# Other tiles for the second weight halves, for the b12 parts and for the first block's products in a stick-breaking decoder block

## The chip, the cores and the metric

The kernel runs on one core of one Trainium2 chip. The metric is the time of one execution in microseconds of the device. The kernel before has a median of 2233.52 us over three runs (2228.97, 2233.52 and 2234.57).

The core's engines are TensorE (PE, matmuls), VectorE (DVE), ScalarE (ACT), GpSimd (POOL) and SyncE (SP, which here issues nearly all DMAs). Each works through its own list of instructions in order and waits on semaphores for the others.

## The reference

One decoder block, 2048 tokens of width 1024, all in float32:

```
h = rmsnorm(x, g_mix_pre) * (1 + scale_m) + shift_m
mix = concat(stick_breaking_attention(q, k, v), pooling(u)) @ w_out     # q, k, v, u = h @ w_in
x = x + gate_m * rmsnorm(mix, g_mix_post)
h = rmsnorm(x, g_ffn_pre) * (1 + scale_f) + shift_f
f = (silu(h @ w_gate) * (h @ w_up)) @ w_down                            # 1024 -> 2816 -> 1024
x = x + gate_f * rmsnorm(f, g_ffn_post)
```

The change touches only the feed-forward part, from `h @ w_gate` and `h @ w_up` on.

## The kernel before, in words

**Precision.** A float32 product is made of three matmuls of rounded parts: each operand is split into a high part (ScalarE's rounding copy) and a low part (VectorE's difference), and `mm3` (lines 72 to 74) multiplies high by high, low by high and high by low. In the feed-forward part the split often goes through a PSUM bank (`split_by_bank`: L1169 the high part, L1176 a copy of it, L1177 the difference). A step of the plan is one group of such matmuls into one PSUM bank.

**Fast matrix products.** The feed-forward products `h @ w_gate` and `h @ w_up` are cut into 2 x 2 blocks (tokens by halves, features by halves, sums by halves), and are made by a Strassen-Winograd scheme in two levels: fewer block products, more additions of operands and results. The outer level has seven products. Four of them are made by an inner scheme of seven products each: these are the four groups `q` = 0 to 3 of `inner` (p1 to p4), each with 11 positions `j`, a position for 128 + 128 columns of gate and up. A position has seven steps of six matmuls, called a, e, f, b, h, i and d after their banks; d is put behind the first step of the next position. The other three outer products are made by `gate_up`, in 11 blocks of 12 steps with 12 matmuls each (`t_g`, `t_u`, `b_g`, `b_u` in the trace), which also takes up the four groups' results, makes silu and the product of gate and up, and the sums that the last product needs. Then `down` multiplies by `w_down` in the same manner, twice, and finishes the rows.

**The order of the work.** All steps stand in one list. The position m (0 to 43) of `inner` begins at step 7m - 1; `gate_up` begins at step 307. Each step carries what has to be done a number of steps ahead of it (`ahead`: loads, sums on GpSimd) and what is done with its bank one or two steps later (`take`). Beside the list a "side" generator makes the operands of the coming group, a piece a step: `main_operands` beside the fourth group, `rest_operands` from step 307 on. The order on TensorE, ScalarE, VectorE and GpSimd is the program's order. SyncE's DMAs are put in an order by the planner, which follows its own estimate of when each can go; on the chip that order is fixed, so a DMA that waits holds all behind it.

**Tiles.** Tiles come from pools by tag. A tag has a fixed number of buffers (`FT` for the pool `fx`); a new tile of a tag waits until an older one's last reader is done. What matters here:
- "s", six buffers: the results `p_c` of `inner` (`done`, L1384), which `keep` (L1380) stores two steps later to the DRAM tensor `pd`. In `rest_operands` four of them also hold b12 parts.
- "w320" and "w321" in the pools `ring` and `fx`: raw weights. Group q == 3 needs sums of two halves of the rows of the weights. The first halves (loaded at L1331) rotate over three tiles; the second halves (L1339) all go to one, "w321" of `ring`, but for the last position, whose second halves go to the two "cu" tiles. `row_sum` (L1342, GpSimd) adds the second half into the first, 10 steps (gate) and 9 steps (up) ahead of the position; the loads are issued 16 steps ahead. `s12` and `s34` (L1354 to L1360, GpSimd) follow at 8 and 7.
- "gf", one buffer of double width: a wide tile for several uses. "u2" and "u3", two buffers each: results of `take_p6` and `take_p7`, in `inner` and in `gate_up`.
- "gs" (three), "cu" (two), "u4" and "p1" (one each): token parts `hs` loaded by `token_part` (L1615) and intermediate results.
- `products_load` (L1426) loads four results of the groups from `pd`, 1 MB at once, into tiles `px` that rotate over "yah", "yal" and "y22", which until then hold operands of the fourth group.

The first gate/up block takes its weights (L1438) 21, 20, 17 and 11 steps ahead: gate's into both raw tiles of `ring`, up's into both of `fx`. In that block the first results are taken up in `take_p6`, where `u2g` (L1490) adds the first matmuls and a product from `px`. Five PSUM banks rotate there; bank 0 was the one of the last d step of the fourth group.

`down` (its slots of "u2" and "u3", and its load of `gfd` into "gf") and `combine` and `down_sums` are the rest of the code that the change's tiles touch.

Of the kernel before, what the change touches and what calls it, by code (L numbers as in the profile page):

```python
# [17 lines left out]
P = 128  # L18
# [3 lines left out]
HK = KC // 2  # L22
# [6 lines left out]
TB = 512  # L29
# [3 lines left out]
LAG = 2  # L33
OFF = 7
PRB = 6
FT = {"tr": 1, "gs": 3, "u4": 1, "gf": 1, "sr": 4, "s": 6, "u2": 2, "w320": 1, "u3": 2, "w321": 1, "p1": 1, "cu": 2}
WIDE = {"tr": 4, "gf": 2, "w320": 2, "w321": 2}
PAIRS, MAIN_PAIRS, HELD = 6, 4, 4
HELD_AT = (20, 12)
NQ = 4  # L40
# [7 lines left out]
def block_kernel(ctx, tc, x, c, w_cond, b_cond, g_mix_pre, g_mix_post, w_in, w_pool,  # L48
                 pool_scale, w_out, g_ffn_pre, g_ffn_post, w_gate, w_up, w_down, out):
    nc = tc.nc  # L50
# [1049 lines left out]
    for n in range(len(steps) + OFF):  # L1100
# [4 lines left out]
        if n < len(steps):  # L1105
            u, i = steps[n]
# [207 lines left out]
    def inner(q, j):  # L1314

        p = f"p{q + 1}"
        name = f"{p}_{j}"
        m = HF * q + j
        st = {}

        def load():
            if m == 0:
                st["g"], st["u"], st["s12"], st["s34"] = (t[:, n] for t in raw_pair(ring, name, (P, 2, TB)) for n in range(2))
            else:
                turn = 0 if m == 1 else (31 - m) % 4
                pool, n = ((fx, 1), (ring, 0), (fx, 0))[m % 3] if m >= 30 else (ring if turn > 1 else fx, turn % 2 == 0)
                w = ft("gf", f"{name}_32", (P, 2, TB)) if m == NQ * HF - 1 else raw_tile(pool, n, name, (P, 2, TB))
                st["g"], st["u"] = w[:, 0], w[:, 1]
            k0, f = ((0, j), (HK, j), (HK, j + HF), (0, j + HF))[q]
            for n, src in (("g", w_gate), ("u", w_up)):  # L1330
                (nc.scalar if m in (4, 5) else nc.sync).dma_start(st[n].rearrange("p (k n) -> p k n", k=HK), rows_of(src, k0, f))  # L1331
            if q == 3:
                if m == NQ * HF - 1:
                    st["g2"], st["u2nd"] = (ft("cu", f"{name}_2{n}") for n in "gu")
                else:
                    w = raw_tile(ring, 1, f"{name}_2", (P, 2, TB))
                    st["g2"], st["u2nd"] = w[:, 0], w[:, 1]
                for n, src in (("g2", w_gate), ("u2nd", w_up)):
                    nc.sync.dma_start(st[n].rearrange("p (k n) -> p k n", k=HK), rows_of(src, HK, f))  # L1339

        def row_sum(n, other):
            nc.gpsimd.tensor_tensor(st[n], st[n], st[other], ALU.add)  # L1342

        half = TB // 2
        one, two = slice(0, half), slice(half, TB)

        def sum_tile(n):
            if n not in st:
                st[n] = ft("sr", f"{name}_{n}")
            return st[n]  # L1350

        def s12():
            t, g, u = sum_tile("s12"), st["g"], st["u"]
            nc.gpsimd.tensor_tensor(t[:, one], u[:, one], u[:, two], ALU.add)  # L1354
            nc.gpsimd.tensor_tensor(t[:, two], t[:, one], g[:, one], ALU.subtract)

        def s34():
            t, g, u = sum_tile("s34"), st["g"], st["u"]
            nc.gpsimd.tensor_tensor(t[:, one], g[:, one], u[:, one], ALU.subtract)
            nc.gpsimd.tensor_tensor(t[:, two], g[:, two], st["s12"][:, two], ALU.subtract)  # L1360

        def step(w, part, v, vpart, bank, after, split_first=True):

            def split_w():
                if split_first:
                    pair = operand(f"{name}_{w}")
                    cols = two if w == "u" else slice(0, TB)
                    split_by_bank(*(t[:, cols] for t in pair), st[w][:, cols])
                    st[w + "r"] = [x.rearrange("p (k n) -> p k n", k=HK) for x in pair]

            def mm():
                st[bank] = (e_ps if bank in "de" else p_ps)(f"{bank}{name}")
                (wh, wl), (th, tl) = st[w + "r"], ys[p][v]
                mm3(st[bank], [((wh[:, 2 * part + k, :], wl[:, 2 * part + k, :]), (th[:, 2 * vpart + k, :], tl[:, 2 * vpart + k, :]))
                               for k in range(2)])

            return Step(1, split_w, mm, [(1, do) for do in after])

        def keep(kind, sb, t):
            nc.sync.dma_start(pd[sb][:, j, q // 2 * 4 + 2 * kind + q % 2, :], t)  # L1380

        def done(kind, sb, ps, rest):
            t = ft("s", f"{name}_c{kind}{sb}")
            nc.vector.tensor_tensor(t, ps, rest, ALU.add)  # L1384
            later(2, lambda: keep(kind, sb, t))

        def take_p1():
            st["p1"] = ft("p1", f"p1{name}")
            nc.scalar.copy(st["p1"], st["a"])

        def take_p5():
            st["u4"] = t = ft("gf" if not q and m and m % 2 == 0 else "u4", f"u4{name}")
            if not q:
                nc.scalar.copy(t, st["e"])

        def take_p6():
            st["u2"] = ft("u2", f"u2{name}")
            nc.vector.tensor_tensor(st["u2"], st["f"], st["p1"], ALU.add)
            if q:
                nc.vector.tensor_tensor(st["u4"], st["e"], st["u2"], ALU.add)  # L1400
            else:
                nc.gpsimd.tensor_tensor(st["u4"], st["u4"], st["u2"], ALU.add)

        def take_p7():
            st["u3"] = ft("u3", f"u3{name}")
            nc.vector.tensor_tensor(st["u3"], st["h"], st["u2"], ALU.add)

        r = [step("g", 0, "ya", 0, "a", [take_p1]),
             step("s12", 0, "v14", 0, "e", [take_p5]),
             step("s12", 1, "v32", 1, "f", [take_p6], False),  # L1410
             step("g", 1, "ya", 1, "b", [lambda: done(0, 0, st["b"], st["p1"])], False),
             step("s34", 0, "v32", 0, "h", [take_p7, lambda: done(1, 1, st["e"], st["u3"])]),
             step("u", 1, "v14", 1, "i", [lambda: done(1, 0, st["i"], st["u3"])]),
             step("s34", 1, "y22", 0, "d", [lambda: done(0, 1, st["d"], st["u4"])], False)]
        r[0].ahead = [({1: 9, 2: 12}.get(m, 16 if q == 3 else 14), load), (5 if m == 1 else 8, s12), (4 if m == 1 else 7, s34)]
        if q == 3:
            r[0].ahead += [(10, lambda: row_sum("g", "g2")), (9, lambda: row_sum("u", "u2nd"))]
        return r
# [2 lines left out]

    def products_load(n, sb, j):

        tag, pool = (("yah", "0r"), ("yal", "0r"), ("y22", "0b"))[next(px_turn) % 3]
        px[n, sb, j] = opools[pool].tile([P, 4, TB], F32, tag=tag, bufs=1, name=f"px{n}{sb}_{j}")
        nc.sync.dma_start(px[n, sb, j], pd[sb][:, j, 4 * n:4 * n + 4])  # L1426

    px_turn = itertools.count()

# [31 lines left out]
    def gate_up(j, at):  # L1461
# [24 lines left out]

        def take_p6(kind, sb, ps):
            p1, p2 = to_bank(0, kind, 0, sb), first(0, kind, 1, sb)
            u2 = st["u2", kind, sb] = ft("u2" if kind == "g" else "u3", f"u2{kind}{sb}_{j}")
            nc.vector.tensor_tensor(u2, ps, first(0, kind, 0, sb), ALU.add)  # L1490
            if kind == "g":
                gate("a11", sb, "sr", p1, p2)
            else:
                up("a11", sb, p1, p2)
# [115 lines left out]
                yield  # L1610
                yield

    def token_part(n, T0, tag, i):
        t = ft(tag, f"hs{T0}_{i}_{n}", (P, HK, P))
        nc.sync.dma_start(t, h2d[T0 + n % 2 * HK + i][:, n // 2 * HK:(n // 2 + 1) * HK, :])  # L1615
        return t

# [53 lines left out]
    def main_operands():  # L1671
# [18 lines left out]

        for u in range(2 * HK):
            t = 6 + 8 * u if u < 7 else 66
            tags = ("cu", "cu", "gf") if u in (1, 3, 5) else ("gs",) * 3
            for n, k, tag in zip((1, 3, 0), (6, 6, 5), tags):
                at(max(t - k, 0), lambda u=u, n=n, tag=tag: load(u, n, tag))
            at(t, lambda u=u: add(u, 1, 3, ALU.subtract))
            at(t + 1, lambda u=u: add(u, 0, 1, ALU.add))
            if u < HK:
                at(t + 2, lambda u=u: place(u, 1, "t3"))
                at(t + 4, lambda u=u: place(u, 3, "b22"))  # L1700
            at(t + 3 + 3 * (u < HK), lambda u=u: place(u, 0, "t2"))
# [5 lines left out]
    def rest_operands():  # L1707

        ops[1].update({n: pair_of(opools["0b"], tag, f"{n}_1") for n, tag in (("t3", "v14"), ("b22", "v32"))})
        b12 = [token_part(1, NTS, "s", i) for i in range(HK)]  # L1710
        b22 = [token_part(3, NTS, tag, i) for i, tag in enumerate(("gs", "gs", "gs", "p1"))]
        yield
        yield
        for k in range(HK + 2):
# [6 lines left out]

    def down(sb, dn):
        st = {}
        slots = ["s"] * 4 + ["u2", "u2", "u3", "u3"]
        wd_rows = w_down.rearrange("(i j p) n -> i p j n", p=P, i=2)
        quads = []

# [433 lines left out]
```

## Time and profile before

| | us |
|---|---|
| median of three runs | 2233.52 |
| lowest, highest | 2228.97, 2234.57 |
| profiled execution, its time | 2234.14 |
| its span, first to last instruction | 2232.4 |
| TensorE busy | 2180.1 (98%) |
| VectorE busy | 1669.8 (75%) |
| ScalarE busy | 1356.4 (61%) |
| GpSimd busy | 1217.4 (55%) |

The profile is of one execution. A line L72 in it is line 72 of the kernel file; since helpers record most matmuls, the tile's name tells which product it is (`ap` is bank a of a position, `t_g` a step of `gate_up`). In a line of the waits stand who waited, for whom, the total, the number of times and the longest. In a line in order of time stand the start, the duration, the engine, the line, the operation and output<-inputs, and in brackets the idle time before it and what ended it. Matmuls are pipelined: they are shown with 0.39 us each, though they begin every 0.23 us. SPq is SyncE's queue of DMA issues; its durations are those of the issue, not of the transfer.

### The profile page before, as it was taken

The page shows a single profiled execution, that of the slowest core. Times are in us where ns is not written, and L with a number is a line of the kernel's source. Part 1 is how long each engine was busy: PE and PEld are TensorE (multiplying, and loading weights), DVE is VectorE, ACT ScalarE, POOL GpSimd, SP SyncE. Part 2 cuts the span into 40 slices and gives each one's busy share as a digit, 9 for nine tenths or more (in the row PEclk, how much of TensorE's full clock was granted, in tenths as well). Part 3 has the DMA queues.
Part 4 walks back from the last instruction along what each step waited for, and adds up shares of the span by engine and source line. Part 5 has one row for each costly group of instructions (what it writes and reads, how often), then busy time and mean ns, then how long its engine had stood idle before and what let it go on. Part 6 is the DMA issues. An engine that isn't in the chain of part 4 may idle for free.

```text
span 2232.4 us, 34290 instructions
## 1 busy us (share of the span) xinstructions
PE 2180.1 (98%) x10349; PEld 1794.5 (80%) x10349; DVE 1669.8 (75%) x2552; ACT 1356.4 (61%) x2796; POOL 1217.4 (55%) x1700
## 2 busy tenths in 40 slices
PE   8999999999999999999999998799999999999998
PEld 6888888888888888878878876678888888887887
DVE  7874499999999965557787766597788775576566
ACT  5435599898989844457676655464444444455444
POOL 1452277787779965548887666556665520033003
PEclk9999999999999999999999999999999999999999
DMA  9986886534444456678899767889999997679553
GB/s 315 350 277 210 286 207 176 154 105 116 123 119 104 144 174 201 209 239 271 279 319 320 265 215 232 296 296 303 314 315 299 305 330 258 209 244 322 183 199 122
DMA packets 365622, 524.78 MB, mean 235 GB/s; under 512 B 24503, under 2 KB 204283, under 8 KB 357629
## 3 DMA queue, kind: packets, MB, share of 16 engines
q1 hardware_dynamic: 362876, 521.02, 71.7%
q8 instruction: 82, 1.34, 0.3%
q10 hardware_dynamic: 2560, 1.58, 0.3%
q14 instruction: 104, 0.84, 0.1%
HBM read 350.01 MB, written 172.49 MB: 234 GB/s over the span
## 4 chain that ended last, share of the span: by engine, by line
PE 45%; DMA 4%; DVE 4%; POOL 2%; issue 2%; ACT 2%; SPq 0%; DVEq 0%; POOLq 0%; ACTq 0%
PE dn0p L72 3%; PE dn0p L74 3%; PE dn0p L73 3%; DMA pd<-p_c 3%; PE dn1p L73 2%; PE dn1p L74 2%; PE dn1p L72 2%; PE t_u L74 2%; PE t_u L73 2%; PE t_u L72 2%; PE t_g L73 2%; PE t_g L72 2%; PE t_g L74 2%; PE mix L72 1%; PE mix L74 1%
## 5 line engine op out<-in xcount | busy, mean ns | idle before, releaser
L953 POOL TENSOR_TENSOR w<-sg,pr 128x512 f32<-128x512 f32 (+2 forms) x320 | 306.8, 959 | 46.1 <-DVE pr L948 13.5
L948 DVE TENSOR_TENSOR_SCAN pr<-pr,carry,begin 128x512 f32<-128x512 f32 x192 | 243.9, 1271 | 0.0
L932 ACT ACTIVATE sg<-z 128x512 f32<-128x512 f32 (+2 forms) x320 | 183.0, 572 | 50.9 <-PE z L930 40.5
L63 DVE TENSOR_TENSOR wtl<-wt,wth 128x512 fp32r<-128x512 f32 (+1 forms) x320 | 189.5, 592 | 17.9 <-ACT wth L62 15.8
L62 ACT CAST wth<-wt 128x512 fp32r<-128x512 f32 (+1 forms) x320 | 181.8, 568 | 10.4 <-PE wt L964 8.0
L934 ACT ACTIVATE pr<-z 128x512 f32<-128x512 f32 (+2 forms) x320 | 182.1, 569 | 0.0
L964 PE MATMUL wt<-ident,w 128*128 128x128 f32 x1088 | 172.3, 273 | 1.6 <-POOL pr L944 1.1
L964 PEld LDWEIGHTS wt<-ident,w 128*128 128x128 f32 x1088 | 134.0, 140 | 32.8 <-POOL pr L944 1.9
L1479 ACT ACTIVATE sa<-sa 128x512 f32<-128x512 f32 x88 | 54.9, 633 | 166.0 <-DVE sa L1478 162.6
L979 PE MATMUL av<-wth,vt 128*128 128x512 f32 (+1 forms) x320 | 126.1, 394 | 0.9 <-ACT o L984 0.8
L72 PE MATMUL dn0p<-w0p_h,g0p_h 128*128 128x512 f32 x308 | 119.8, 389 | 0.0
L73 PE MATMUL dn0p<-w0p_l,g0p_h 128*128 128x512 f32 x308 | 119.8, 389 | 0.0
L74 PE MATMUL dn0p<-w0p_h,g0p_l 128*128 128x512 f32 x308 | 119.8, 389 | 0.0
L929 PE MATMUL z<-kt,qt 128*128 128x512 f32 (+2 forms) x320 | 118.6, 371 | 0.7 <-ACT pr L934 0.6
L63 DVE TENSOR_TENSOR g0p_l<-g0p,g0p_h 128x512 fp32r<-128x512 f32 x77 | 59.3, 771 | 80.0 <-ACT g0p_h L62 80.0
L980 PE MATMUL av<-wtl,vt 128*128 128x512 f32 (+1 forms) x320 | 117.8, 368 | 1.3 <-DVE wtl L63 1.2
L930 PE MATMUL z<-kt,qt 128*128 128x512 f32 (+2 forms) x320 | 117.0, 366 | 0.0
L72 PE MATMUL dn1p<-w1p_h,g1p_h 128*128 128x512 f32 x292 | 113.7, 389 | 1.1 <-ACT w1p_h L62 1.1
L73 PE MATMUL dn1p<-w1p_l,g1p_h 128*128 128x512 f32 x292 | 113.8, 390 | 0.3 <-DVE w1p_l L63 0.3
L74 PE MATMUL dn1p<-w1p_h,g1p_l 128*128 128x512 f32 x292 | 113.6, 389 | 0.0
L945 DVE TENSOR_TENSOR_SCAN pr<-pr,zero,begin 128x128 f32<-128x128 f32 (+3 forms) x128 | 111.1, 870 | 1.7 <-ACT pr L934 1.7
L62 ACT CAST g0p_h<-g0p 128x512 fp32r<-128x512 f32 x77 | 48.0, 623 | 105.3 <-PE dn0p L73 90.3
(844 smaller groups left out, 7154.2 us busy)
## 6 DMA issues: line engine op xcount, KB each, us to landing
pd<-p_c SPq DMA_DIRECT2D x176, 256.0 KB, 4.8
px<-pd SPq DMA_DIRECT2D x44, 1024.0 KB, 7.3
hs<-h2d SPq DMA_DIRECT2D x80, 256.0 KB, 4.9
wc<-in_w_cond_dram SPq DMA_DIRECT2D x32, 512.0 KB, 7.4
qt<-qd SPq DMA_DIRECT2D x64, 256.0 KB, 4.0
p<-in_w_gate_dram SPq DMA_DIRECT2D x52, 256.0 KB, 4.9
p<-in_w_up_dram SPq DMA_DIRECT2D x52, 256.0 KB, 5.3
kt<-kd SPq DMA_DIRECT2D x96, 128.0 KB, 3.3
```

The costliest lines, as they stand in the source:

```text
L62: nc.scalar.copy(hi, src)
L63: low.tensor_tensor(lo, src, raw(hi), ALU.subtract)
L72: nc.tensor.matmul(ps, lh, rh, start=first and i == 0, stop=False)
L73: nc.tensor.matmul(ps, lh, rl, start=False, stop=False)
L74: nc.tensor.matmul(ps, ll, rh, start=False, stop=last and i == n - 1)
L929: nc.tensor.matmul(z[:, 0:L], qt[:, 0, i * P:(i + 1) * P], keys, start=True, stop=False)
L932: nc.scalar.activation(sg[:, 0:L], z[:, 0:L], AF.Sigmoid, scale=0.125)
L934: nc.scalar.activation(pr[:, 0:L], z[:, 0:L], AF.Sigmoid, scale=-0.125)
L948: nc.vector.tensor_tensor_scan(keys, keys, begin, carry, ALU.mult, ALU.bypass)
L953: nc.gpsimd.tensor_tensor(w[:, 0:L], sg[:, 0:L], pr[:, 1:L + 1], ALU.mult)
L964: nc.tensor.transpose(wt[:, i * P:(i + 1) * P], wss[u][i][:, b * P:(b + 1) * P], ident)
L979: nc.tensor.matmul(av[:, lo0:], vb, wh[:, lo0:], start=first, stop=False)
```

## The change

- The second weight halves of group q == 3 alternate: odd positions use "w321" of `ring`, even ones "gf" of `fx`; now the last position but one (m = 42) uses the two "cu" tiles, and the last (m = 43) "w321" of `ring`. Its first half stays in "gf".
- Of the four loads of a position in that group, the two of gate come first, then the two of up; before, the two first halves came first.
- `rest_operands` puts the b12 parts in one "cu" tile, two halves of a "gf" tile and "u4" instead of four "s" tiles, and issues each b12 load together with its b22 load.
- `products_load` begins its rotation with "yal" instead of "yah", and the loads with j = 0 and n = 0 (one for each half of the tokens) are made in two pieces of 512 KB.
- "u2" and "u3" have one buffer each, and "v2" and "v3" are new with one each. `inner` uses "u2" and "u3" alone; `gate_up` uses u for the first and v for the second half of the tokens; `down` uses all four; `main_operands` puts three of its parts in "v2" that were in "gf".

```diff
-FT = {... "u2": 2, "w320": 1, "u3": 2, ...}
+FT = {... "u2": 1, "v2": 1, "w320": 1, "u3": 1, "v3": 1, ...}
@@ inner, load
-            for n, src in (("g", w_gate), ("u", w_up)):
-                (nc.scalar if m in (4, 5) else nc.sync).dma_start(st[n].rearrange("p (k n) -> p k n", k=HK), rows_of(src, k0, f))
+            parts = [("g", w_gate, k0), ("u", w_up, k0)]
             if q == 3:
-                if m == NQ * HF - 1:
+                if m == NQ * HF - 2:
                     st["g2"], st["u2nd"] = (ft("cu", f"{name}_2{n}") for n in "gu")
                 else:
-                    w = raw_tile(ring, 1, f"{name}_2", (P, 2, TB))
+                    w = raw_tile(ring, 1, f"{name}_2", (P, 2, TB)) if m % 2 else ft("gf", f"{name}_2", (P, 2, TB))
                     st["g2"], st["u2nd"] = w[:, 0], w[:, 1]
-                for n, src in (("g2", w_gate), ("u2nd", w_up)):
-                    nc.sync.dma_start(st[n].rearrange("p (k n) -> p k n", k=HK), rows_of(src, HK, f))
+                parts = [parts[0], ("g2", w_gate, HK), parts[1], ("u2nd", w_up, HK)]
+            for n, src, k in parts:
+                (nc.scalar if m in (4, 5) else nc.sync).dma_start(st[n].rearrange("p (k n) -> p k n", k=HK), rows_of(src, k, f))
@@ products_load
-        tag, pool = (("yah", "0r"), ("yal", "0r"), ("y22", "0b"))[next(px_turn) % 3]
+        tag, pool = (("yal", "0r"), ("yah", "0r"), ("y22", "0b"))[next(px_turn) % 3]
-        nc.sync.dma_start(px[n, sb, j], pd[sb][:, j, 4 * n:4 * n + 4])
+        for k in range(0, 4, 2 if j + n < 1 else 4):
+            m = slice(k, k + (2 if j + n < 1 else 4))
+            nc.sync.dma_start(px[n, sb, j][:, m], pd[sb][:, j, 4 * n + m.start:4 * n + m.stop])
@@ gate_up, take_p6
-            u2 = st["u2", kind, sb] = ft("u2" if kind == "g" else "u3", f"u2{kind}{sb}_{j}")
+            u2 = st["u2", kind, sb] = ft("uv"[sb] + "23"[kind == "u"], f"u2{kind}{sb}_{j}")
@@ token_part
-    def token_part(n, T0, tag, i):
-        t = ft(tag, f"hs{T0}_{i}_{n}", (P, HK, P))
+    def token_part(n, T0, tag, i, t=None):
+        t = ft(tag, f"hs{T0}_{i}_{n}", (P, HK, P)) if tag else t
@@ main_operands
-            tags = ("cu", "cu", "gf") if u in (1, 3, 5) else ("gs",) * 3
+            tags = ("cu", "cu", "v2") if u in (1, 3, 5) else ("gs",) * 3
@@ rest_operands
-        b12 = [token_part(1, NTS, "s", i) for i in range(HK)]
-        b22 = [token_part(3, NTS, tag, i) for i, tag in enumerate(("gs", "gs", "gs", "p1"))]
+        b12, b22 = [], []
+        wide = ft("gf", "hs_wide", (P, 2, HK, P))
+        for i, (tag, tag2) in enumerate((("cu", "gs"), (None, "gs"), (None, "gs"), ("u4", "p1"))):
+            b12.append(token_part(1, NTS, tag, i, wide[:, (i - 1) % 2]))
+            b22.append(token_part(3, NTS, tag2, i))
@@ down
-        slots = ["s"] * 4 + ["u2", "u2", "u3", "u3"]
+        slots = ["s"] * 4 + ["u2", "v2", "u3", "v3"]
```

More of the change, by code (lines that the diff above doesn't have):

```diff
@@ L35 @@
 PRB = 6
-FT = {"tr": 1, "gs": 3, "u4": 1, "gf": 1, "sr": 4, "s": 6, "u2": 2, "w320": 1, "u3": 2, "w321": 1, "p1": 1, "cu": 2}
+FT = {"tr": 1, "gs": 3, "u4": 1, "gf": 1, "sr": 4, "s": 6, "u2": 1, "v2": 1, "w320": 1, "u3": 1, "v3": 1, "w321": 1, "p1": 1, "cu": 2}
 WIDE = {"tr": 4, "gf": 2, "w320": 2, "w321": 2}
```

## The prediction, as it went on record

> **What bounds the kernel now.** I read the page first, then the busy times by stretch, then the waits of TensorE, VectorE and SyncE's queue inside the weak stretch, then the time order of each engine there.
>
> ```profile
> span 2232.4 us, 34290 instructions
> PE 2180.1 (98%) x10349; PEld 1794.5 (80%) x10349; DVE 1669.8 (75%) x2552; ACT 1356.4 (61%) x2796; POOL 1217.4 (55%) x1700
> PE   8999999999999999999999998799999999999998
> ```
>
> TensorE is the bound. All that any edit outside the matmuls can win is its idle time, and the slices show where a lump of it lies, in the 8 and the 7 of slices 25 and 26 of 40. By stretches:
>
> ```profile
> 1140.00:1280.00 140.00, 140.00 (x619) 115.95 (x618) 112.53 (x187) 93.82 (x179) 105.75 (x118) 1.00 0.91 304
> 1280.00:1305.00 25.00, 23.36 (x101) 18.51 (x101) 17.63 (x30) 14.76 (x28) 19.57 (x22) 1.00 0.65 210
> 1305.00:1431.00 126.00, 111.65 (x466) 86.42 (x464) 82.25 (x136) 67.61 (x127) 78.28 (x80) 0.99 0.72 233
> 1431.30:1443.40 12.10, 12.10 (x53) 10.00 (x54) 4.30 (x7) 5.09 (x8) 3.00 (x3) 1.00 1.05 393
> 1443.40:1452.90 9.50, 0.39 (x2) 0.03 (x1) 0.84 (x2) 2.60 (x5) 6.89 (x6) 0.63 0.91 307
> ```
>
> The columns are length, then busy time with count of PE, PEld, DVE, ACT, POOL, then granted clock, DMA share and GB/s. From 1140 to 1280 (the second and third group of FFN products) PE never stops. From 1305 to 1431 lies the fourth group (q == 3), and PE is busy only 111.65 of 126; at 1443.4 it stands still for 9.5 us in the first gate/up block.
>
> ```profile
> 1305.54 0.39 PE L72 MATMUL ap<-yap4h,p_g_h 128*128 128x512 f32 x1
> ...
> 1314.83 0.39 PE L74 MATMUL ip<-v14p4h,p_u_l 128*128 128x512 f32 x1
> ...
> 1431.27 0.47 PE L72 MATMUL t_g<-t_0h,g_s_h 128*128 128x512 f32 x1 [0.53 <-DVE p_c L1384]
> ...
> 1443.40 0.39 PE L74 MATMUL t_u<-t_1h,u_s_l 128*128 128x512 f32 x1
> 1452.90 0.77 PE L72 MATMUL t_g<-t_0h,g_s_h 128*128 128x512 f32 x1 [9.11 <-DVE p_c L1384]
> ...
> 1457.23 0.39 PE L72 MATMUL t_u<-t_0h,u_s_h 128*128 128x512 f32 x1
> ```
>
> The first two rows are matmuls 1 and 42 of one position: 9.29 us over 41 spacings, 0.2266 us each, so a step of six takes 1.36 us and a position of seven steps 9.52 us. Four losses follow.
> - Tail of the third group: 25.0 us for 101 matmuls that need 22.9: 2.1 us.
> - Fourth group: 11 positions of 42 are 462 matmuls, 104.7 us; from 1305.54 to 1431.27 it took 125.7: 21.0 us.
> - Standstill: the matmul at 1443.40 should be followed at 1443.63; the next starts at 1452.90: 9.3 us.
> - Slow clock behind it: 12 matmuls from 1452.90 to 1457.23 take 4.33 us where 2.72 are due: 1.6 us.
>
> Together 34.0 us, the most that can go. Who causes them:
>
> ```profile
> SPq L1339 <- POOL p L1342: 39.1, 9, 6.5
> DVE p_c L1384 <- DMA pd<-p_c: 42.2, 14, 10.1
> POOL p L1342 <- DMA p<-in_w_gate_dram: 13.5, 4, 4.6
> POOL p L1342 <- DMA p<-in_w_up_dram: 10.5, 4, 6.0
> ```
> ```profile
> 1290.93 0.44 SPq L1380 DMA_DIRECT2D pd<-p_c  x1
> 1296.74 0.38 SPq L1339 DMA_DIRECT2D p<-in_w_gate_dram  x1
> 1297.21 0.93 SPq L1380 DMA_DIRECT2D pd<-p_c  x2
> 1298.20 0.49 SPq L1339 DMA_DIRECT2D p<-in_w_up_dram  x1
> ```
>
> Waits of 1280 to 1460 (total, times, longest). L1339 loads the second weight halves into one tile. Each load waits until GpSimd's row sum (L1342) of the position before has read it; SyncE's queue is in order, so the stores of the products (L1380) stand behind it, as between 1290.93 and 1296.74. The product tiles (tag "s", six) then don't come free, VectorE's next `p_c` waits, and with it the PSUM bank that PE wants. Nine holds of 39.1 us go with 2.1 + 21.0 us of loss: 0.59 us per us held.
>
> ```profile
> 1437.36 6.27 SPq L1615 DMA_DIRECT2D hs<-h2d  x5
> ...
> 1444.79 1.66 SPq L1380 DMA_DIRECT2D pd<-p_c  x1
> ```
> ```profile
> 1440.63 0.69 DVE L1490 TENSOR_TENSOR u2g<-t_g,px 128x512 f32<-128x512 f32 x1 [4.31 <-DMA px<-pd]
> 1452.06 0.69 DVE L1384 TENSOR_TENSOR p_c<-dp,u4p 128x512 f32<-128x512 f32 x1 [10.13 <-DMA pd<-p_c]
> ```
>
> The standstill has the same tail and another head: four of the six "s" tiles are given to b12 parts, so the last `p_c` must wait for a store that goes out at 1444.79, behind the `hs` loads. Its bank, 0, is what the next `t_g` needs.
>
> **The change, part by part.** The sum is made against the profiled execution's 2234.14 us, 0.03% above the median 2233.52.
>
> *Two tiles for second halves* (odd positions ring, even ones "gf", the last but one "cu"). A load now waits for the sum two positions earlier, 9.52 us more of slack against a longest hold of 6.5: the nine holds go, and 23.1 us with them. What is late next? At full pace the group's busy shares become POOL 78.28/104.7 = 75%, DVE 79%, ACT 65%, DMA 233 x 126/104.7 = 280 GB/s; from 1140 to 1280, with PE never idle, they are 76%, 80%, 67% and 304. No engine becomes the bound.
>
> *Gate's halves first.* The four issues and the stores between them took 3.7 us (1296.74 to the end of the last load issue); gate's pair is now out in about the first 1. Landing and sums:
>
> ```profile
> DMA to landing us min/median/max: 3.0/4.5/5.6
> L1342 POOL TENSOR_TENSOR p<-p,p x20: 1269/1291/1309, 1294.2 to 1399.6; 128x512 f32<-128x512 f32 x20
> ```
>
> The sums stand 6 and 7 steps behind the load, 8.2 and 9.5 us: gate's is due 6 to 7 us after the first issue, up's 8 to 9. It fits, up's barely; I count nothing gained here.
>
> *Two holds stay.* The "cu" pair for position 42 (step 277) was last read by an add that the side generator issues at the end of that same step; and the gate weights of the first block (step 286) now share the ring tile with position 43, whose sum stands at step 291. I take 2 us a hold, near one and a half steps of lag (0 if other work is queued ahead, 6.5 as before at worst): 2 x 2 x 0.59 = 2.4 us come back, 0 to 7.7.
>
> *b12 in "cu", "gf" and "u4".* "s" holds products alone, so the last `p_c` no longer waits for a store behind `hs` loads: 9.3 + 1.6 us go. The loads keep their number; five of eight find their tile free ahead of the block, the one in "u4" only after the last `p_c`, which frees it. What is late next for bank 0: VectorE is in order, and `u2g` waits for the products until 1440.63; that, one more addition and `p_c`, three of 0.69 us, end near 1442.7, still ahead of 1443.63.
>
> *First block's products in halves, tiles swapped.* Two more issues of about 0.5 us on SyncE; half of the bytes stand ahead of `u2g`. Swapping the tiles moves a release by one matmul (0.23 us). Counted at nothing: the 0.9 us between 1442.7 and 1443.63 cover the issues, and without that cover they cost their 1.0.
>
> *"v2" for the third main tile, "u2" and "u3" split.* In gate/up the rotation is as before. In the 44 positions u2 and u3 now have one buffer instead of two.
>
> ```profile
> L1398 DVE TENSOR_TENSOR u2p<-fp,p1p x11: 678/692/692, 993.2 to 1087.8; 128x512 f32<-128x512 f32 x11
> L1402 POOL TENSOR_TENSOR u4p<-u4p,u2p x11: 1289/1297/1312, 994.6 to 1088.7; 128x512 f32<-128x512 f32 x11
> ```
>
> GpSimd's reads start 0.9 to 1.4 us after the first and last writes and take 1.3; the next write is some 9.5 us off: no wait. This is the one read by another engine, and only the first group has it.
>
> *A new wait at the seam.* Weights, `hs` parts and products crowd there (393 GB/s). I take one wait of about 0.7 us, with a clock dip, whose price these rows give:
>
> ```profile
> 1328.86 0.47 PE L72 MATMUL ap<-yap4h,p_g_h 128*128 128x512 f32 x1 [1.86 <-DVE u2p L1398]
> ...
> 1329.88 0.63 PE L73 MATMUL ap<-yap4l,p_g_h 128*128 128x512 f32 x1
> ...
> 1332.87 0.57 PE L74 MATMUL dp<-y22p,p_s_l 128*128 128x512 f32 x1
> ```
>
> Seven spacings take 2.99 us instead of 1.59, 1.4 us lost behind a wait of 1.86. So 0.7 + 1.4 = 2.1 us (0 to 2.1 + 1.6). [...]
>
> Sum: 34.0 - 2.4 - 2.1 = 29.5 us; 2234.14 - 29.5 = **2204.6 us**.
>
> **Rivals.**
> - *The seam is bound by transfers.* During the standstill 9.5 us x 307 GB/s = 2.9 MB moved. If they are all needed without it, at 393 GB/s they take 7.4 us, with the dip 1.6: 2200.1 + 2.4 + 9.0 = 2211.5. For it: DMA share 1.05 ahead of the standstill. Against: five `hs` loads move ahead of the block, into a stretch with share 0.72.
> - *The fourth group is paced by landing.* GpSimd's 24.0 us of waits for weights (13.5 + 10.5) then stay. If up's sum is late by 1.5 us in each of 11 positions, 11 x 1.5 x 0.59 = 9.7 us stay: 2200.1 + 9.7 + 4.5 = 2214.3. For it: up's margin is under 1.5 us. Against: the loads go out on time once the queue isn't held.
> - *The holds move elsewhere.* SyncE's order is set by the planner; if `hs` loads waiting for "gs", "cu" or the shared ring tile hold the stores as L1339 did, the gain shrinks to a few us: about 2230.
> - *Slower: single u2.* In the first group VectorE's next write of u2 waits for GpSimd's read of the last. A wait of x in each of its 11 positions costs 11x; from x = (34.0 + 6.7)/11 = 3.7 us on the kernel is slower, at 4.5 us it takes 2200.1 + 4.5 + 49.5 = 2254. For it: GpSimd is in order, and a wait there for weights delays the read. Against: the read would have to end over 10 us later than the rows show. Elsewhere writer and readers are VectorE alone.
>
> **How the numbers follow.** Chances: forecast 0.62; transfers 0.17; landing 0.12; holds move 0.06; slower 0.03. A measurement of this kernel tells some 0.3% (6.7 us) from no change: the first three are faster (0.91), the fourth within (0.06), the last slower (0.03). The range runs from 2198 (all 34.0 gone and 0.1% of run to run) to 2215, which takes in the two middle rivals; outside are the last two and the edges, under 0.2.
>
> **What would show it.** Right: the wait of L1339 for L1342 near nothing; the waits of `p_c` for its stores fall from 42.2 to under 10 us; fourth group near 105 us; no wait of `t_g` for `p_c` of 9 us. The landing rival would show L1342 still waiting over 15 us for weights; the transfer rival a PE wait of several us in the first block for `px`, `hs` or weights with DMA share near 1; the slower one a wait of L1398 for L1402. I am wrong if the fourth group still takes over 115 us, or if PE loses time in a place where it does not today.

## The result and the profile after

The kernel after takes 2225.76 us (median of 16 runs, 2223.70 to 2228.95); the kernel before, beside it, 2234.52 us (16 runs). The ratio is 0.9961, with a 95% interval of 0.9954 to 0.9969. It is faster by 8.8 us where 29.5 were forecast, and lies above the range of 2198 to 2215. The profiled execution took 2223.88 us.

The page after, its span and TensorE's row of slices:

```profile
span 2222.1 us, 34293 instructions
PE   8999999999999999999999999899999999999998
```

Of the 8 and the 7 in slices 25 and 26 one 8 is left. Next come the stretches after (length, then busy time with count of PE, PEld, DVE, ACT, POOL, then granted clock, DMA share, GB/s): the tail of the third group, the fourth group, and the seam to the first gate/up block.

```profile
1280.00:1305.00 25.00, 23.04 (x99) 17.87 (x98) 17.85 (x30) 14.74 (x28) 19.80 (x22) 1.00 0.66 218
1305.00:1431.00 126.00, 112.38 (x466) 86.16 (x464) 81.32 (x135) 67.47 (x127) 77.44 (x79) 0.99 0.71 228
1431.00:1457.00 26.00, 23.89 (x103) 19.25 (x103) 20.02 (x31) 17.17 (x30) 12.02 (x10) 1.00 1.06 368
```

The seam is nearly full now. Before, the same stretch read:

```profile
1431.00:1457.00 26.00, 16.62 (x66) 13.34 (x67) 9.50 (x17) 10.43 (x17) 10.72 (x9) 0.80 0.92 325
```

37 matmuls more are 37 x 0.2266 = 8.4 us: nearly the whole gain of 8.8. The fourth group kept its 112 busy us of 126. The first matmul of the group and the first behind it, after:

```profile
1305.64 0.39 PE L72 MATMUL ap<-yap4h,p_g_h 128*128 128x512 f32 x1
...
1431.99 0.47 PE L72 MATMUL t_g<-t_0h,g_s_h 128*128 128x512 f32 x1 [0.99 <-DVE p_c L1384]
```

They stand 126.35 us apart, where before it was 125.7 and 104.7 were due. The waits after, from 1280 to 1460 (total, times, longest):

```profile
SPq L1339 <- POOL p L1342: 38.1, 7, 7.0
DVE p_c L1384 <- DMA pd<-p_c: 38.7, 17, 5.2
```

The hold that the second tile was to remove is there with 38.1 us in 7 waits, against 39.1 in 9. The time order shows why. In SyncE's queue before, L1339 is a load of second halves and L1331 one of first halves:

```profile
1296.74 0.38 SPq L1339 DMA_DIRECT2D p<-in_w_gate_dram  x1
...
1298.78 0.56 SPq L1331 DMA_DIRECT2D p<-in_w_gate_dram  x1
...
1307.01 0.37 SPq L1339 DMA_DIRECT2D p<-in_w_gate_dram  x1
...
1310.23 0.40 SPq L1331 DMA_DIRECT2D p<-in_w_gate_dram  x1
...
1319.08 0.38 SPq L1339 DMA_DIRECT2D p<-in_w_gate_dram  x1
```

After, the same queue (all four loads are now of line 1339; the second, 1298.86, and the fourth, 1309.91, are first halves), and GpSimd's row sums:

```profile
1296.82 0.38 SPq L1339 DMA_DIRECT2D p<-in_w_gate_dram  x1
...
1298.86 0.56 SPq L1339 DMA_DIRECT2D p<-in_w_gate_dram  x1
...
1306.75 0.37 SPq L1339 DMA_DIRECT2D p<-in_w_gate_dram  x1
...
1309.91 0.38 SPq L1339 DMA_DIRECT2D p<-in_w_gate_dram  x1
...
1319.26 0.38 SPq L1339 DMA_DIRECT2D p<-in_w_gate_dram  x1
```
```profile
1294.26 2.54 POOL L1342 TENSOR_TENSOR p<-p,p 128x512 f32<-128x512 f32 x2
1304.04 2.68 POOL L1342 TENSOR_TENSOR p<-p,p 128x512 f32<-128x512 f32 x2 [4.22 <-DVE p_s_l L1177]
...
1327.44 1.27 POOL L1342 TENSOR_TENSOR p<-p,p 128x512 f32<-128x512 f32 x1 [2.69 <-DMA p<-in_w_gate_dram]
...
1396.85 1.30 POOL L1342 TENSOR_TENSOR p<-p,p_2g 128x512 f32<-128x512 f32 x1 [5.44 <-DVE u2p L1398]
```

The issues stand at the same times to a few tenths; what they load is different. The order of the built program on SyncE names it, for the positions j = 0 to 3 of the group (gate's loads alone; "2nd" are second halves, in brackets what a load waits for, beside others):

```
before   1st j=0 | 2nd j=1 [sum of j=0] | 1st j=1 | 2nd j=2 [sum of j=1] | 1st j=2 | 2nd j=3 [sum of j=2] | 1st j=3
after    1st j=0 | 2nd j=2 [sum of j=0] | 1st j=1 | 2nd j=3 [sum of j=1] | 1st j=2 | 2nd j=4 [sum of j=2] | 1st j=3
```

(After, the second halves of j = 1 stand some 80 entries ahead of those of j = 0, and no sum holds them.) With two tiles a load of second halves waits for the sum two positions back. But the planner, which puts a load where it reckons its tile to come free, now places it one position earlier on the list. It still stands before the sum that is just being made, and the next position's first halves stand behind it, as before. So a ring is closed: a sum ends at 1306.72 (1304.04 and 2.68), the second halves go out at 1306.75, the first halves behind them at 1309.91, they land, and the next sums follow; the two of the next position end near 1319.2, and at 1319.26 the queue moves again. The brackets of GpSimd's rows name now the first halves (1327.44), now a VectorE operation. The landings settle it: of the positions 1 to 9 the trace has the landing of gate's first halves for j = 1, 5, 6, 8 and 9, and each time the sum begins 0.12 or 0.13 us later (j = 1: landed at 1303.91, begun at 1304.04). From the first gate sum to the tenth the ring takes (1396.85 - 1294.26)/9 = 11.40 us a position, where the matmuls need 9.52: 11 x 11.40 = 125.4 us, the length of the group.

### The profile page after: what moved, and what is told of

Same layout as the page of the kernel before. It is cut to its first block, busy times and chain, and to the rows that moved or that the text cites. A ratio compares the mean times of both kernels' runs of the same rounds, so it can differ in the third digit from the quotient of the medians.

```text
span 2222.1 us, 34293 instructions
## 1 busy us (share of the span) xinstructions
PE 2179.7 (98%) x10349; PEld 1794.8 (81%) x10349; DVE 1673.5 (75%) x2552; ACT 1355.9 (61%) x2796; POOL 1215.6 (55%) x1700
## 4 chain that ended last, share of the span: by engine, by line
PE 77%; DVE 6%; DMA 5%; POOL 4%; issue 3%; ACT 3%; SPq 1%; DVEq 0%; POOLq 0%; ACTq 0%
PE wt L964 4%; PE dn0p L73 3%; PE dn0p L74 3%; PE dn0p L72 3%; PE dn1p L72 3%; PE dn1p L73 3%; PE dn1p L74 3%; PE av L980 2%; PE z L929 2%; PE z L930 2%; PE av L979 2%; DMA pd<-p_c 2%; PE mix L72 2%; PE mix L74 2%; PE mix L73 2%
```

## The experiments

What was left to tell apart: does the order on SyncE (the loads behind the hold, the first halves above all) make the group slow, or do the stores behind the hold, as the prediction had it, or is one tile simply too few? And which of the three parts of the change brought the 8.8 us? Each run is compared with the kernel before on its own chip (medians 2232.65, 2233.08 and 2233.83). In the code shown, ... stands for lines left out.

**The parts alone.** Each is the kernel before with one part of the change.

`tiles_only`: the second halves on two tiles, gate's first, with "v2" and "v3".

```diff
...
-w = raw_tile(ring, 1, f"{name}_2", (P, 2, TB))
+w = raw_tile(ring, 1, f"{name}_2", (P, 2, TB)) if m % 2 else ft("gf", f"{name}_2", (P, 2, TB))
...
+parts = [parts[0], ("g2", w_gate, HK), parts[1], ("u2nd", w_up, HK)]
...
```

> The kernel before with the second weight halves on two tiles, gate's first, and with u2, v2, u3, v3 (main's three parts in v2); b12 parts and products as before. Theory A (the planner puts each load of second halves where its tile comes free in its own estimate, so a second tile moves the load one position earlier and SyncE still stands before it until the row sum just being made is done): no gain, 2232 to 2237 us, the fourth group still near 126 us, L1339 waiting some 38 us for L1342. Rival B (the two tiles do relieve the group, and the rest of the change gives it back): 2210 to 2220 us.

2237.06 us, ratio 1.0019 (1.0010 to 1.0029). The second tile alone gains nothing; if anything it costs 4 us, and what costs them stays open. Its waits from 1280 to 1460:

```profile
SPq L1339 <- POOL p L1342: 38.9, 7, 6.2
PE t_g L72 <- DVE p_c L1384: 9.2, 1, 9.2
```

Both losses of before are there.

`b12_only`: the b12 parts in "cu", "gf" and "u4".

```diff
-b12 = [token_part(1, NTS, "s", i) for i in range(HK)]
...
+wide = ft("gf", "hs_wide", (P, 2, HK, P))
+for i, (tag, tag2) in enumerate((("cu", "gs"), (None, "gs"), (None, "gs"), ("u4", "p1"))):
+    b12.append(token_part(1, NTS, tag, i, wide[:, (i - 1) % 2]))
...
```

> The kernel before with the b12 parts in cu, gf and u4, issued beside the b22 parts, and nothing else. Theory A: the whole gain of the change is here, 2224 to 2228 us, no wait of 9 us of t_g for p_c. Rival C (the standstill goes only if the products come earlier too): 2229 to 2234 us with a wait of u2g for px in its place.

2224.17 us, ratio 0.9967 (0.9956 to 0.9979): the gain of the whole change, within the interval.

```profile
SPq L1339 <- POOL p L1342: 37.1, 9, 6.7
PE t_g L72 <- DVE p_c L1384: 0.8, 1, 0.8
```

The hold is as before, and TensorE's 9 us of standstill are gone.

`products_only`: the first block's products in halves, the tiles swapped.

```diff
-(("yah", "0r"), ("yal", "0r"), ("y22", "0b"))[next(px_turn) % 3]
+(("yal", "0r"), ("yah", "0r"), ("y22", "0b"))[next(px_turn) % 3]
...
```

> The kernel before with the first block's products in halves and the tiles yal and yah swapped, nothing else. Theory A: no change, 2232 to 2237 us, the wait of 9 us stays because its store still goes out behind the hs loads. Rival C: 2227 to 2231 us.

2233.95 us, ratio 1.0006 (0.9997 to 1.0015): nothing, as counted.

**What the group could be.** `no_second_halves`: the kernel after without the loads of the second halves and their sums.

```diff
-parts = [parts[0], ("g2", w_gate, HK), parts[1], ("u2nd", w_up, HK)]
...
-r[0].ahead += [(10, lambda: row_sum("g", "g2")), (9, lambda: row_sum("u", "u2nd"))]
```

> The changed kernel without the loads of the second weight halves and without their row sums; this part of the computation is left out, so its time is a floor for the fourth group. Theory A (the hold of SyncE at these loads is what costs): the group takes 105 to 108 us and the kernel 2200 to 2207 us. Rival D (another bound holds the group: the stores, the first halves or the order on VectorE): the group over 115 us, the kernel over 2212 us.

2200.85 us, ratio 0.9867 (0.9850 to 0.9883). The group:

```profile
1304.69 0.39 PE L72 MATMUL ap<-yap4h,p_g_h 128*128 128x512 f32 x1
...
1409.41 0.39 PE L72 MATMUL t_g<-t_0h,g_s_h 128*128 128x512 f32 x1
```

104.7 us, the floor of the prediction: the whole loss of the group hangs on these loads and sums. This run does not say how.

**The order.** `pinned`: the kernel after, with the second halves bound to be issued behind the first halves of their own position. Tiles, bytes and sums stay.

```diff
-parts = [parts[0], ("g2", w_gate, HK), parts[1], ("u2nd", w_up, HK)]
-for n, src, k in parts:
+parts += [("g2", w_gate, HK), ("u2nd", w_up, HK)]
+for i, (n, src, k) in enumerate(parts):
+    with (tc.issue_after(loaded.ins) if i > 1 else ExitStack()):
+        loaded = (...).dma_start(...)
```

> The changed kernel with one more rule for the planner: a position's second halves are issued behind its first halves (issue order only, no wait for data). Theory A (the second tile was spent on issuing a position earlier; held to its place, the load meets a tile whose sum is long done): L1339's and L1340's waits for L1342 under 15 us, the group under 112 us, 2203 to 2212 us. Rival D (one position's sum, landing and next sum make a loop that no order shortens): group over 120 us, 2220 us or more.

2201.95 us, ratio 0.9863 (0.9849 to 0.9878). Its stretch of the fourth group, a wait, gate's loads in its queue (first halves of j = 1 and j = 2, second halves of j = 2, first and second halves of j = 3) and three sums:

```profile
1305.00:1411.00 106.00, 105.61 (x466) 87.21 (x465) 83.09 (x136) 67.94 (x127) 76.77 (x78) 1.00 0.85 269
```
```profile
DVE p_c L1385 <- DMA pd<-p_c: 7.5, 4, 3.3
```
```profile
1292.85 0.79 SPq L1340 DMA_DIRECT2D p<-in_w_gate_dram  x1
...
1300.59 0.38 SPq L1340 DMA_DIRECT2D p<-in_w_gate_dram  x1
...
1302.96 0.39 SPq L1340 DMA_DIRECT2D p<-in_w_gate_dram  x1
...
1307.92 0.38 SPq L1340 DMA_DIRECT2D p<-in_w_gate_dram  x1
...
1309.43 1.16 SPq L1340 DMA_DIRECT2D p<-in_w_gate_dram  x1
```
```profile
1308.80 2.55 POOL L1343 TENSOR_TENSOR p<-p,p 128x512 f32<-128x512 f32 x2 [1.67 <-DVE p_c L1385]
1316.85 2.55 POOL L1343 TENSOR_TENSOR p<-p,p 128x512 f32<-128x512 f32 x2
1325.02 2.56 POOL L1343 TENSOR_TENSOR p<-p,p 128x512 f32<-128x512 f32 x2
```

The first halves of j = 1 go out at 1292.85, where after they went out behind the hold at 1298.86; those of j = 2 at 1300.59 and not at 1309.91. The sums now come 8.1 us apart, faster than the 9.52 that TensorE needs, and TensorE is busy for 105.61 of 106 us. The order alone is worth 2225.76 - 2201.95, about 24 us, or 22.4 when each is taken against the kernel before of its own batch.

`by_scalar_queue`: the kernel after, with the second halves issued by ScalarE. Their wait then holds nothing on SyncE.

```diff
-(nc.scalar if m in (4, 5) else nc.sync).dma_start(...)
+(nc.scalar if m in (4, 5) or n in ("g2", "u2nd") else nc.sync).dma_start(...)
```

> The changed kernel with the second halves issued by ScalarE's queue, in program order, 16 steps ahead of the position, instead of SyncE's. Theory A: SyncE has no hold left there; group 105 to 110 us, 2201 to 2209 us. Rival E (the issue and its wait only move onto ScalarE, whose casts then come late): 2212 us or more, with waits of PE for the casts or copies of L1169 and L1176.

2203.15 us, ratio 0.9867 (0.9853 to 0.9882); the group takes 104.7 us (1307.24 to 1411.96). The same gain in another way. The time of the issues alone does not make it: the 22 issues moved last 10.2 us together, the longest being

```profile
1361.18 0.75 ACTq L1339 DMA_DIRECT2D p<-in_w_up_dram  x1
```

and 22.6 us are saved against the kernel after (21.2 when each is taken against the kernel before of its own batch), because what stood behind the wait no longer does: on SyncE no wait of L1339 for L1342 is left from 1280 to 1460, where after there were 38.1 us of it.

`first_halves_written_first`: the kernel after with both first halves written ahead of the second halves in the program, as before, and nothing bound.

```diff
-parts = [parts[0], ("g2", w_gate, HK), parts[1], ("u2nd", w_up, HK)]
+parts += [("g2", w_gate, HK), ("u2nd", w_up, HK)]
```

> The kernel after with one edit: in the program both first halves of a position are written ahead of both second halves again, with nothing that binds the planner. If the planner places a load where its tile comes free, whatever the order of writing, SyncE's list stays what it is, the fourth group takes 126 us and the time is 2226 us (2223 to 2229). If it was writing gate's pair ahead of up's that put the second halves of a later position in front, the group falls to 105 to 115 us and the time to 2202 to 2214.

2225.25 us, ratio 0.9959 (0.9946 to 0.9971): the order of writing changes nothing. The planner places the loads, and of the edit of `pinned`, which writes them in this order too, the binding is what gains.

**Stores or loads behind the hold.** `stores_by_scalar`: the kernel after with the fourth group's stores on ScalarE's queue. SyncE's holds then keep back only loads.

```diff
-nc.sync.dma_start(pd[sb][:, j, q // 2 * 4 + 2 * kind + q % 2, :], t)
+(nc.scalar if q == 3 else nc.sync).dma_start(pd[sb][:, j, q // 2 * 4 + 2 * kind + q % 2, :], t)
```

> The changed kernel with the fourth group's stores of products issued by ScalarE's queue; the loads stay on SyncE, held as before. Theory S (the cost comes through the stores behind the hold, the s tiles and p_c): waits of p_c for pd under 10 us, group under 112 us, 2203 to 2212 us. Theory F (it comes through the next position's first halves behind the hold: sum, issue, landing, next sum make a loop of 11.5 us): the group stays over 120 us, 2219 to 2228 us, and PE waits for s12 or the gate split instead of for p_c.

2227.23 us, ratio 0.9974 (0.9964 to 0.9983), no better than after. Waits, then SyncE's gate loads (second halves, first halves, second halves, from 1339 on), then the sums and two `hs` additions of GpSimd (L1687), which make operands for `gate_up`:

```profile
SPq L1339 <- POOL p L1342: 40.2, 9, 6.8
DVE p_c L1384 <- DMA pd<-p_c: 7.9, 4, 3.7
```
```profile
1339.50 0.37 SPq L1339 DMA_DIRECT2D p<-in_w_gate_dram  x1
...
1341.62 0.45 SPq L1339 DMA_DIRECT2D p<-in_w_gate_dram  x1
...
1351.32 0.37 SPq L1339 DMA_DIRECT2D p<-in_w_gate_dram  x1
```
```profile
1336.96 2.50 POOL L1342 TENSOR_TENSOR p<-p,p 128x512 f32<-128x512 f32 x2 [0.41 <-DVE p_s_l L1177]
...
1347.53 1.30 POOL L1687 TENSOR_TENSOR hs<-hs,hs 128x512 f32<-128x512 f32 x1 [1.21 <-DMA hs<-h2d]
1348.78 2.52 POOL L1342 TENSOR_TENSOR p<-p,p 128x512 f32<-128x512 f32 x2
...
1358.20 2.66 POOL L1687 TENSOR_TENSOR hs<-hs,hs 128x512 f32<-128x512 f32 x2 [3.87 <-DMA hs<-h2d]
1360.82 2.52 POOL L1342 TENSOR_TENSOR p<-p,p 128x512 f32<-128x512 f32 x2
```

VectorE's waits for stores fell from 38.7 to 7.9 us, and the kernel gained nothing: the sums still come 11.8 and 12.0 us apart, with no store on SyncE in these rows. So the stores behind the hold are not needed for the slow pace; the loads behind it are enough. This run does not part one kind of load from the other. At 1348.78 and 1360.82 gate's first halves had landed 0.5 and 1.2 us before the sum began, and what ended last was an `hs` addition, whose load is behind the hold as well. That the first halves set the pace in the kernel after is shown there, by their landings. The run is no clean one in two more respects: the last stores of the third group stay on SyncE until 1324, and ScalarE, with 44 issues more, now makes VectorE wait for its copies (15.9 us of `p_s_l`). The group takes 130.5 us (1306.16 to 1436.64), so its length is no measure of the hold alone. The rows used here are of the time after 1324.

**One tile or two.** `one_tile_pinned`: the kernel before, with one tile for the second halves, and the same binding of the order.

```diff
...
+with tc.issue_after(loaded.ins):
     nc.sync.dma_start(st[n].rearrange("p (k n) -> p k n", k=HK), rows_of(src, HK, f))
```

> The kernel before (one tile) with the same rule of issue order. Theory A (with one tile the sum just being made must still be awaited: hold, loads, landing of some 5 us, two sums of 1.3): the hold stays, group 115 to 126 us, 2224 to 2236 us. Rival F (only the first halves behind the hold cost): group under 112 us, 2214 to 2221 us, the standstill of 9 us at the seam left.

2208.14 us, ratio 0.9886 (0.9870 to 0.9903), faster than either expectation. The group takes 104.7 us (1302.50 to 1407.22); the standstill is left:

```profile
PE t_g L72 <- DVE p_c L1385: 7.8, 1, 7.8
```

`b12_one_tile_pinned`: the same with the b12 parts in the tiles of the change. `pinned_second_look` ran beside it, with the edit of `pinned`.

> The kernel before with two edits: the b12 parts in the tiles of the change, and the second halves of a position issued behind its own first halves. One tile for the second halves stays. If the place on SyncE's list is all that the fourth group needs, the second tile is worth nothing: the group takes 105 us, the standstill of 9 us is gone too, and the time is that of the pinned kernel, 2202 us (2200 to 2204). If the second tile does carry a part of the gain once the order is right (landing and the row sum then come one after the other in one tile), it is 2205 to 2212, with waits of GpSimd's row sum for the weights over 15 us and TensorE idle in the fourth group.

> The kernel after with the second halves issued behind their own position's first halves, as in the run pinned, beside the two others on the same chip: 2202 us (2200 to 2204). If the one-tile kernel of this batch is within 3 us of it, the second tile is worth nothing that can be measured here.

One tile: 2199.04 us, ratio 0.9844 (0.9831 to 0.9858). Two tiles, with the rest of the change: 2200.78 us, ratio 0.9853 (0.9839 to 0.9867). The intervals overlap; the second tile is worth nothing that can be measured. In the one-tile kernel the fourth group has no gap at all, though its sums still wait for gate's weights:

```profile
1305.00:1411.00 106.00, 106.00 (x469) 87.79 (x468) 83.89 (x138) 70.40 (x131) 79.26 (x80) 1.00 0.89 286
```
```profile
POOL p L1343 <- DMA p<-in_w_gate_dram: 14.6, 7, 5.4
```

This is the fastest kernel of the study: 34.8 us below the kernel before, two edits to it, one of them (the b12 parts) from the change.

## Why the prediction was wrong, step by step

- **The losses of before, 34.0 us: right.** With both causes gone (`b12_one_tile_pinned`) the gain is 34.8 us.
- **"A load now waits for the sum two positions earlier ... the nine holds go, and 23.1 us with them": wrong, and this is the step that failed.** The first half of it holds; the second does not follow. It took the load's place in the queue as given and let only its tile come free earlier. The planner moved the load forward by the same position, so the hold stayed (38.1 us) and the 23.1 us with it. What was needed could be read in the text's own words, that SyncE's order is the planner's; it was used for a rival about `hs` loads alone.
- **The chain from hold to TensorE: wrong in its middle.** The prediction went from the held stores over the "s" tiles to `p_c`. That wait is real but not what binds: with most of it gone (`stores_by_scalar`) the sums come no faster. What binds goes from the held first halves over the row sum back to the next hold. The size, 23.1 us for the tail and the group, was nearly right: the order brings 2224.17 - 2199.04 = 25.1 us between two kernels that differ in it alone, each in its own batch.
- **Standstill and slow clock, 9.3 + 1.6 us, by the b12 parts: right.** `b12_only` gains 8.5 us by itself, near the 10.9 less the 2.1 us of the next point.
- **A new wait at the seam, 2.1 us: right in size, by luck.** The stretch from 1431 to 1457 has PE busy for 23.89 of 26 us, so it is idle for 2.1. The forecast was made of one wait of 0.7 us and a clock dip of 1.4; the granted clock is 1.00 there, and TensorE waits three times, 0.99 us for `p_c` (at 1431.99; before it was 0.53) and 0.46 and 0.91 us for the coming operand `t_1` (at 1455.83 and 1457.24). By the count of matmuls, 103 where 26 us hold 114.7, the loss is 2.7 us.
- **"Two holds stay", 2.4 us: void,** since nearly all stayed. Both waits are in the trace after, and longer than the 2 us that were forecast for each: the "cu" pair waits for `hs` additions (L1339 for L1687, 6.3 us in two waits), and the first block's gate load waits for the sum in the shared ring tile (L1440 for L1342, 3.5 us; before, as L1438 for L1342, 3.8 us, so this one is not new). What the "cu" pair costs by itself was not tried.
- **Gate's halves first, the products in halves, single "u2": nothing gained, right.** Only the products were tried alone (`products_only`). For "u2" no wait of L1398 for L1402 stands in the first group's waits after. Gate's halves first and the split of "u2" and "u3" are in `tiles_only`, and whether its 4 us come from one of them is not known.
- **The rivals.** "The holds move elsewhere" (0.06, about 2230) came nearest, with the wrong place, since the hold stayed at its line, and a price some 4 us too high, since the standstill's gain is independent of it. Landing as the limit falls: the sums wait 14.6 us for gate's weights in the fastest kernel, and TensorE never waits for them. Transfers at the seam fall too: the seam lost 2.1 to 2.7 us and not the 9.0 of that rival.

## What to carry to other kernels

A second buffer gives slack only if the load stays where it was in its queue; where a scheduler places loads by when their tile comes free, it may spend the buffer on an earlier issue, and the wait stands in front of the same neighbours as before (here 38.1 us of holds with two tiles, 39.1 with one). Before counting a hold as gone, write down the new order of that queue and ask what each waiting entry has behind it. Here the cure was to bind the order (what is needed first goes first), and it worked with one buffer (2199.04 us) as well as with two (2200.78 us); moving the waiting loads to another queue, tried with two buffers, worked nearly as well (2203.15 us).

## What the runs showed of the hardware

The clock's dip does not go by the length of the wait alone. In the kernel after, TensorE's rows around two waits:

```profile
1328.97 0.47 PE L72 MATMUL ap<-yap4h,p_g_h 128*128 128x512 f32 x1 [1.90 <-DVE u2p L1398]
...
1330.83 0.63 PE L73 MATMUL dp<-y22p,p_s_h 128*128 128x512 f32 x1
...
1333.82 0.41 PE L74 MATMUL ep<-v14p4h,p_s_l 128*128 128x512 f32 x1
```
```profile
1413.39 0.47 PE L72 MATMUL ep<-v14p4h,p_s_h 128*128 128x512 f32 x1 [2.74 <-DVE p_c L1384]
1413.70 0.40 PE L73 MATMUL ep<-v14p4l,p_s_h 128*128 128x512 f32 x1
...
1416.69 0.39 PE L74 MATMUL bp<-yap4h,p_g_l 128*128 128x512 f32 x1
```

Behind 1.90 us of waiting, and only after 1.5 us of full speed, seven spacings take 2.99 us instead of 1.59; the granted clock is 0.50 from 1330.4 to 1333.8. Behind 2.74 us of waiting 13 spacings from 1413.70 take 2.99 us, full speed, with a granted clock of 1.00. What else decides whether the clock dips, these rows do not show.
